# Batch-norm matmul on one core: the stores of seventeen output blocks are issued from ScalarE's queue instead of SyncE's

## The chip, the cores and the metric

One core of a Trainium2 chip runs the kernel. The metric is the device time of one execution in microseconds, the median of three runs. Engines are named as in the profile: PE (TensorE, matmuls), PEld (its weight loads), DVE (VectorE), ACT (ScalarE), POOL (GpSimd), SP (SyncE). An engine's instructions run in the order in which they stand in its queue. A transfer is issued by an instruction in the queue of SP, ACT or POOL, and 16 DMA engines then move the data.

## The reference

```python
y = np.matmul(x, weight)                        # (16, 512, 1024) x (1024, 768)
mean = np.mean(y, axis=(0, 1), keepdims=True)
var = np.var(y, axis=(0, 1), keepdims=True)
y_norm = (y - mean) / np.sqrt(var + eps)
return (gamma * y_norm + beta).astype(np.float32)
```

The input is 8192 rows of 1024 float32; the output is 8192 rows of 768 columns in float32, 25.2 MB. Mean and variance of a column go over all 8192 rows, so no value of a column can be stored before the last row has gone through the matmul for it.

## The kernel before

**Work.** The 768 columns are six column tiles of 128, the rows 16 chunks of 512. x and the weights are loaded as bfloat16 through POOL's queue; DVE turns x so that the contracted dimension lies on the partitions (xT_sb). For some chunks ACT and DVE make a second copy with even and odd elements apart (x_pl, L547). Column tiles 0 and 1 are computed with rows on the partitions (L510) while x comes in. Tiles 2 to 5 are computed with columns on the partitions (L575): chunks 0 to 3 early, the other twelve when x is complete, tile after tile. Eight matmuls fill one PSUM bank with a 128x512 result.

**Eviction.** Each such bank is read twice: DVE takes its statistics (L711), then ACT casts it to bfloat16 in SBUF (y_sb, L715). After that the bank is free for PE. PSUM has eight banks in turn; some hold other things for a time (the spread scale and shift rows a_ps, turned blocks o_ps).

**Finish of a column tile.** When its statistics are complete, DVE and ACT work out scale and shift, and the tile's blocks of 1024 rows are normalised in place, by ACT for tile 2 (L1023), by DVE for tiles 3 and 4 (L1026). A block must be turned back to rows before it is stored, in one of these ways:

- "xact": a DMA transpose from SP's queue (L1220), then ACT casts the turned bfloat16 block to float32 in a ring buffer in SBUF (L1232), then a store of 512 KB (L1202). Thirteen blocks of tiles 2 and 3.
- "pe": PE transposes the block 128x128 at a time into a PSUM bank (L1044, placed between matmuls), ACT copies it to float32 in the ring (L1210), then the same store (L1202). Four blocks of tile 4.
- "raw": the block is turned before normalisation by a DMA transpose (L1106), DVE multiplies it by the spread scale row (L1174), POOL adds the shift row (L1178), and SP stores it (L1182). Six blocks. For each tile with raw blocks the rows are spread by DVE (L1141, L1142) and by four small and three larger copies (L1145), on POOL or ACT as the planner chooses, then ACT puts them into a PSUM bank (L1158).
- Tiles 0 and 1 go out over L937, L942 and the store L946, all without a turn.

The tables in the code count column tiles from 0; the functions below serve tiles 2, 3 and 4.

**Tail.** The last block of tile 4 is held back (L1252, L1255). Tile 5 ends with two half chunks (L753); its statistics are closed at once, ACT takes the root (L1311), DVE normalises (L1348), PE turns (L1044), ACT copies to o_sb (L1361) and SP stores (L1364): 4 MB in eleven stores.

**Order.** Nothing of the order is left to a compiler. Every piece of work is a Task with a priority, a table of engines with two times (how long it occupies the engine, and when its result is there), its dependences and its buffers. `arrange` (L122) plays these times forward: it takes the engine that can begin first and gives it the ready task with the lowest priority number, and a task with several possible engines goes where it can begin first. `slack` is added to the time at which a task counts as ready. Transfers go through a model of the DMA engines with a list of landings for each queue (`Wires`, L98), which lets at most eight be under way on a queue. The instructions are then emitted in the order found, and each engine keeps it (`seq`, L293). So a changed time or engine of one task can move other tasks, also on engines that the change does not name. Waits are made from the data: an instruction waits on semaphores for what it reads or overwrites.

The functions with the stores of this change are `col_block` and those in it, quoted here as they stand before.

Of the kernel before, what the change touches and what calls it, by code (L numbers as in the profile page):

```python
# [227 lines left out]
def kernel(  # L228
# [19 lines left out]
    P = 128  # L248
# [44 lines left out]
    def seq(bi):  # L293

        ins = bi.ins
        prev = last.get(ins.engine)
        if prev is not None:
            tc.add_manual_dep(
                ins, prev,
                mybir.DependencyInfo(mybir.DependencyClass.NoSync, mybir.DependencyReason.DATA),  # L300
                reason="order",
            )
        last[ins.engine] = ins.name
        return bi
# [51 lines left out]
    def task(prio, engines, emit, deps=(), lock=False, **kw):  # L356
        t = Task(prio, engines, emit, deps, **kw)
        t.lock = lock
        tasks.append(t)
        return t  # L360

    def dve(occ):
        return {"DVE": (occ, occ + 0.09)}

    def act(occ):
        return {"ACT": (occ, occ + 0.11)}
# [8 lines left out]
    STORE, XBAR = 1 / 350.0, 1.25  # L375

    def piece(slot):
        return ring[:, slot.at:slot.at + slot.words]
# [69 lines left out]
    for kind, n, *n1 in order:  # L448
# [12 lines left out]
        if m0 == M // 2:  # L461
            affine_loads = affine = task(t, {"SP": (5.0, 7.0)}, load_affine, [x_ready[m0 // CH - 3, 0, JW]])
        slot = Slot(rings, rows // 32 * KQ // 2)
# [4 lines left out]
            dma=(rows * K * 4 / 1024 + 384 * also) * PER_KB * 1.024, takes=[slot])  # L468
# [4 lines left out]
        for i in range(rows // QR):  # L473
            c, q = divmod(m0 // QR + i, QPC)
            for j0, j1 in ((0, JW // 2), (JW // 2, JW)) if m0 < CH else ((0, JW),):
# [4 lines left out]
                    uses=[slot] if new else [slot, x_slot[c]], takes=[x_slot[c]] if new else [])  # L480
# [204 lines left out]
    def y_of(nt, c):  # L685
        return y_col.setdefault((nt, c // GY), Slot(ys))

    def y(nt, c, n=1):
        group = y_of(nt, c).y.rearrange("p g m -> p (g m)")
        return group[:, c % GY * CH:(c % GY + n) * CH]  # L690
# [328 lines left out]
    def norm(nt, c, n=1):  # L1019
        def emit(eng):  # L1020
            part = y(nt, c, n)
            if eng == "ACT":
                seq(nc.scalar.activation(  # L1023
                    part, part, AF.Identity, bias=shift[:, nt:nt + 1], scale=scale[:, nt:nt + 1]))
            else:
                seq(nc.vector.tensor_scalar(  # L1026
                    part, part, scale[:, nt:nt + 1], shift[:, nt:nt + 1],
                    op0=ALU.mult, op1=ALU.add))
        return emit

    def turn_block(prio, nt, m0, count, deps, uses):

        bank = Slot(banks)
        todo = []

        def step():
            if not todo:
                o_ps = psum.tile([P, count, P], bf16, tag="b")
                bank.tile = o_ps
                for s in range(count):  # L1040
                    c, i = divmod(m0 // P + s, RT)
                    todo.append((o_ps[:, s], y(nt, c)[:, i * P:(i + 1) * P]))
            dst, src = todo.pop(0)
            seq(nc.tensor.transpose(dst, src, ident))  # L1044

        def emit(eng):
            for _ in range(emit.task.count):
                step()

        emit.step = step  # L1050
        t = task(prio, pe(0.0555 * count), emit, deps, takes=[bank], uses=uses)
        emit.task = t
        turns[t] = [count, count]
        return t, bank
# [136 lines left out]
    def col_block(nt, c, due, fin_task, held=False):  # L1191
        yslot = y_of(nt, c)
        keeps = [col_end[nt, c + i][1] for i in range(GY)]
        count = GY * RT
        slot = Slot(rings, count * P)
        m0 = c * CH

        def dst():
            return out_flat[m0:m0 + count * P, nt * P:(nt + 1) * P].rearrange("(s p) n -> p s n", p=P)

        def store(eng):
            seq(ENG[eng].dma_start(dst(), slot.o))  # L1202

        a = task(due, act(1.144) if nt == GA else dve(0.45), norm(nt, c, GY), [fin_task] + keeps, nt > GA, uses=[yslot])
        if MODE[nt][c // GY] == "pe":
            b, bank = turn_block(due + 0.5, nt, m0, count, [a], [yslot])

            def copy(eng):
                slot.o = piece(slot).rearrange("p (s n) -> p s n", n=P)
                seq(nc.scalar.copy(slot.o, bank.tile))  # L1210

            d = task(due + 1.0, act(0.905), copy, [b], takes=[slot], uses=[bank])
            task(due + 1.2, {"SP": (0.38, 0.4)}, store, [d], dma=count * P * P * 4 / 1024 * STORE * 1.024,
                 uses=[slot])
            return b
        t_slot = Slot(rings, count * P // 2)

        def xbar(eng):
            t_slot.o = piece(t_slot).bitcast(bf16).rearrange("p (s n) -> p s n", n=P)
            seq(nc.sync.dma_start_transpose(t_slot.o, y(nt, c, GY)))  # L1220

        b = task(due + 0.5, {"SP": (1.4, 1.4)}, xbar, [a], dma=XBAR,
                 takes=[t_slot] + ([slot] if MODE[nt][c // GY] == "xact" else []), uses=[yslot])
        if MODE[nt][c // GY] == "xpool":
            def store_x(eng):
                seq(nc.gpsimd.dma_start(dst(), t_slot.o))

            task(due + 1.2, {"POOL": (0.93, 0.93)}, store_x, [b], dma=1.69, uses=[t_slot])
        else:
            def convert(eng):  # L1230
                slot.o = piece(slot).rearrange("p (s n) -> p s n", n=P)
                seq(nc.scalar.copy(slot.o, t_slot.o))  # L1232

            d = task(due + 1.0, act(0.9), convert, [b], uses=[slot, t_slot])
            d.slack = 1.0
            task(due + 1.2, {"SP": (0.38, 0.4)}, store, [d], dma=count * P * P * 4 / 1024 * STORE * 1.024,
                 uses=[slot])
        return b

    def held_block(nt, c, due, fin_task, last_mm, root_task):  # L1240
# [27 lines left out]
    for nt in range(GA, NT - 1):  # L1268
        if nt == NT - 2:
            for i, c in enumerate(LATE):  # L1270
                part_chunk(c, clock[0] + 0.0 + 4.0 * i, {"DVE": (0.63, 0.7), "ACT": (1.05, 1.1)},
                           i == 0, 4.0 / 4, [col_end[NT - 3, late[-1]][1]])
        for c in CHUNKS[nt]:
            for jws in halves if nt > GA or c > EARLY + 2 else [[jw] for jw in range(JW)]:
                col_unit(nt, c, jws)
        for c in RAW.get(nt, ()):
            if c >= EARLY:
                raw_turn(nt, c, clock[0])
        f = finish_tasks(nt)
        start = clock[0] + 3.0  # L1280
        if nt in RAW:
            raw_spread(nt, f)
        for i in range(C // GY):
            if (nt, GY * i) in raw:
                raw_block(nt, GY * i, start + STEP[nt] * i + RAWDUE[nt])
                continue
            if nt == NT - 2 and C // GY - HELD <= i:
                held.append((nt, GY * i, f))
                continue
            col_block(nt, GY * i, start + STEP[nt] * i, f)  # L1290
# [48 lines left out]
    for c, r0, rows in ends:  # L1339
        due = E + 2.0 + 0.6 * c  # L1340
# [4 lines left out]
        for i in range(n):  # L1345
            def norm_part(eng, c=c + i, r0=r0, rows=min(rows, CH)):
# [5 lines left out]
                              uses=[y_of(nt, c + i)]))  # L1352
        m0 = c * CH + r0
        count = rows // P
        b, bank = turn_block(due + 0.6 * (n - 1), nt, m0, count, norms, [y_of(nt, c + i) for i in range(n)])
        slot = Slot(xts)
# [6 lines left out]
        def store(eng, slot=slot, m0=m0, count=count):  # L1363
# [4 lines left out]
        d = task(due + 0.6 * (n - 1), act(0.05 + 0.107 * count), copy, [b], takes=[slot], uses=[bank])  # L1368
        task(due + 0.6 * (n - 1), {"SP": (0.6, 0.6)}, store, [d], dma=count * P * P * 4 / 1024 * STORE * 1.024,
             uses=[slot])  # L1370
# [41 lines left out]
```

## Time and profile before

| What | Value |
|---|---|
| Device time, median of 3 runs | 205.82 us (205.68 to 205.83) |
| Profiled execution: span from the first to the last instruction | 204.1 us |
| Mean granted TensorE clock over the span | 0.979 |
| PE busy | 189.3 us (93%), 1210 instructions |
| DVE busy | 159.3 us (78%), 250 |
| ACT busy | 146.2 us (72%), 260 |
| POOL busy | 124.1 us (61%), 150 |
| HBM read and written | 36.71 MB and 25.17 MB |
| Stores of 512 KB from the ring on SP's queue | 37, 3.4 us from issue to landing (median) |
| DMA transposes L1220 on SP's queue | 13, 4.4 us from issue to landing (median) |

The profile is of one execution; for that execution there is the span and no separate device time. The span and the median differ by 1.7 us, which lie before the first and behind the last instruction. A group's row gives line, engine, operation, what is written and read, the count, then busy us and mean ns of one, then the engine's idle time before these instructions and what ended most of it. Instructions that issue transfers on SP or ACT are not counted as busy; they appear in the timeline as SPq rows with their own length, from the end of their waits to the end of the issue. In the windows view each row is a stretch of time with the busy us of each engine and the number of instructions in brackets, then the granted clock, the mean busy share of the DMA engines (over 1 where several packets of one engine overlap) and GB/s.

### The profile page before, as it was taken

The page shows a single profiled execution, that of the slowest core. Times are in us where ns is not written, and L with a number is a line of the kernel's source. Part 1 is how long each engine was busy: PE and PEld are TensorE (multiplying, and loading weights), DVE is VectorE, ACT ScalarE, POOL GpSimd, SP SyncE. Part 2 cuts the span into 40 slices and gives each one's busy share as a digit, 9 for nine tenths or more (in the row PEclk, how much of TensorE's full clock was granted, in tenths as well). Part 3 has the DMA queues.
Part 4 walks back from the last instruction along what each step waited for, and adds up shares of the span by engine and source line. Part 5 has one row for each costly group of instructions (what it writes and reads, how often), then busy time and mean ns, then how long its engine had stood idle before and what let it go on. Part 6 is the DMA issues. An engine that isn't in the chain of part 4 may idle for free.

```text
span 204.1 us, 3510 instructions
## 1 busy us (share of the span) xinstructions
PE 189.3 (93%) x1210; PEld 114.5 (56%) x1210; DVE 159.3 (78%) x250; ACT 146.2 (72%) x260; POOL 124.1 (61%) x150
## 2 busy tenths in 40 slices
PE   7969999999999999999999999999999999997900
PEld 3457554657488888777865444444444445544600
DVE  4031879999999999969989998987999878657900
ACT  2001461368989999899978766999998959956950
POOL 7776954877499989997403999389613312940000
PEclk9999999999999999999999999999999999999965
DMA  4999999999999999999686899899999999999998
GB/s 71 172 199 196 176 196 196 196 197 197 190 193 197 197 196 196 196 197 195 103 181 200 297 339 336 248 301 328 295 322 227 336 303 274 347 343 310 310 347 253
DMA packets 98562, 48.74 MB, mean 239 GB/s; under 512 B 24304, under 2 KB 98032, under 8 KB 98544
## 3 DMA queue, kind: packets, MB, share of 16 engines
q0 software_dynamic: 34624, 18.36, 65.5%
q1 hardware_dynamic: 63920, 30.16, 52.6%
q8 instruction: 9, 0.15, 0.3%
q14 instruction: 9, 0.07, 0.1%
HBM read 36.71 MB, written 25.17 MB: 303 GB/s over the span
## 4 chain that ended last, share of the span: by engine, by line
PE 86%; ACT 3%; DMA 3%; POOL 2%; issue 1%; ACTq 0%; DVE 0%; POOLq 0%
PE y_ps L575 54%; PE y_ps L510 24%; PE y_ps L814 4%; ACT o_sb L1361 3%; DMA ring<-in_x_dram 3%; PE o_ps L1044 1%; POOL ring L403 1%; POOL w_sb L387 1%; PE y_ps L753 1%; PE a_ps L903 1%; PE o_ps L1074 0%; ACTq L1407 0%; PE idle_ps L591 0%; PE tot_ps L871 0%; ACT ring L1252 0%
## 5 line engine op out<-in xcount | busy, mean ns | idle before, releaser
L575 PEld LDWEIGHTS <-w_sb 128*128 128x128 bf16 x520 | 50.3, 97 | 57.6
L575 PE MATMUL y_ps<-xT_sb,w_sb 128*128 128x512 bf16 (+1 forms) x272 | 59.3, 371 | 0.0
L575 PE MATMUL y_ps<-x_pl,w_sb 128*128 128x512 bf16 x248 | 57.4, 379 | 0.0
L403 POOL DMA_DIRECT2D ring<-in_x_dram x76 | 47.2, 626 | 14.4 <-DMA ring<-in_x_dram 5.5
L510 PE MATMUL y_ps<-w_sb,xT_sb 128*128 128x256 bf16 x448 | 50.6, 273 | 1.7 <-DMA ring<-in_x_dram 1.6
L510 PEld LDWEIGHTS <-xT_sb 128*128 128x128 bf16 x448 | 43.5, 98 | 9.4 <-DVE xT_sb L435 2.9
L435 DVE STREAM_TRANSPOSE xT_sb<-ring 128x1024 f32<-128x1024 f32 (+1 forms) x29 | 31.2, 1111 | 14.1 <-DMA ring<-in_x_dram 13.9
L711 DVE BATCH_NORM_STATS2 stats<-y_ps 128x6 f32<-128x512 f32 x46 | 30.9, 687 | 7.7 <-PE y_ps L575 7.2
L715 ACT CAST y_sb<-y_ps 128x512 bf16<-128x512 f32 x51 | 29.0, 593 | 10.4 <-DVE stats L711 6.3
L547 ACT COPY x_pl<-xT_sb 128x1024 bf16<-128x1024 bf16 x32 | 32.8, 1063 | 1.7 <-DVE xT_sb L435 1.7
L942 POOL TENSOR_TENSOR ring<-ring,sum 128x1024 f32<-128x1024 f32 (+1 forms) x11 | 23.8, 2188 | 14.9 <-ACT y_ps L724 10.9
L659 ACT ACTIVATE sq_sb<-y_ps 128x512 f32<-128x512 f32 x28 | 16.3, 610 | 16.2 <-PE y_ps L510 15.9
L666 POOL TENSOR_TENSOR sum<-sum,sq_sb 128x512 f32<-128x512 f32 x20 | 25.6, 1278 | 3.0 <-ACT sq_sb L659 1.7
L662 DVE TENSOR_TENSOR sum<-y_ps,sum 128x512 f32<-128x512 f32 x28 | 18.9, 675 | 6.3 <-ACT sq_sb L659 5.3
L672 ACT CAST y_sb<-y_ps 128x512 bf16<-128x512 f32 x28 | 16.3, 594 | 8.2 <-DVE sum L662 8.0
L1178 POOL TENSOR_TENSOR ring<-ring,sum 128x1024 f32<-128x1024 f32 x6 | 14.8, 2477 | 9.8 <-issue 8.5
L937 DVE TENSOR_TENSOR ring<-y_sb,a_ps 128x1024 f32<-128x1024 bf16 (+1 forms) x16 | 16.7, 1079 | 0.1
L1044 PE MATMUL o_ps<-ident,y_sb 128*128 128x128 bf16 x104 | 13.1, 221 | 1.6 <-DVE y_sb L1348 1.5
L1232 ACT CAST ring<-ring 128x1024 f32<-128x1024 bf16 x13 | 13.8, 1063 | 0.6 <-DMA ring<-y_sb 0.6
L1145 POOL COPY sum<-sum 32x256 f32<-32x256 f32 (+1 forms) x17 | 5.8, 340 | 13.4 <-DVE sum L1142 6.5
L428 DVE STREAM_TRANSPOSE xT_sb<-ring 128x2048 bf16<-128x2048 bf16 x6 | 13.5, 2290 | 0.1
L591 PE MATMUL idle_ps<-idle_sb 128*128 128x512 f32 x18 | 9.6, 688 | 1.5 <-DVE idle_sb L316 1.5
(104 smaller groups left out, 153.7 us busy)
## 6 DMA issues: line engine op xcount, KB each, us to landing
out_dram<-ring SPq DMA_DIRECT2D x37, 512.0 KB, 3.4
ring<-in_x_dram POOLq DMA_DIRECT2D x52, 256.0 KB, 8.8
out_dram<-o_sb SPq DMA_DIRECT2D x6, 512.0 KB, 4.7
ring<-in_x_dram POOLq DMA_DIRECT2D x16, 128.0 KB, 5.9
w_sb<-in_weight_dram POOLq DMA_DIRECT2D x8, 192.0 KB, 6.2
out_dram<-ring SPq DMA_DIRECT2D x6, 256.0 KB, 3.0
ring<-in_x_dram POOLq DMA_DIRECT2D x4, 192.0 KB, 7.8
out_dram<-o_sb SPq DMA_DIRECT2D x3, 256.0 KB, 2.5
```

The source lines that it names most:

```text
L403: bi = seq(nc.gpsimd.dma_start(x_bf[32 * i:32 * i + 32], src[:, :, KQ * i:KQ * (i + 1)]))
L435: seq(nc.vector.transpose(dst, src[:, :, jw0:jw1]))
L510: seq(nc.tensor.matmul(y_ps[:, s], x_of(c, jw, e, t * P, (t + 1) * P), w_sb[:, jw, e, 0:NA], start=(s == 0 and jw == 0 and e == 0), stop=( ...
L547: seq(nc.scalar.copy(dst, pairs) if eng == "ACT" else ENG[eng].tensor_copy(dst, pairs))
L575: seq(nc.tensor.matmul(y_ps, w_sb[:, jw, e, nt * P:(nt + 1) * P], moving(c, jw, e, q0 * QR, q1 * QR, parted), start=(jw == 0 and e == 0 an ...
L659: seq(nc.scalar.activation(sq_sb[:, 0:n], slot.tile[:, 0:n], AF.Square))
L662: seq(nc.vector.tensor_add(sum1, slot.tile[:, 0:n], sum1))
L666: seq(ENG[eng].tensor_add(acc, acc, state["sq"][:, 0:n]))
L711: seq(nc.vector.bn_stats(dst, slot.tile))
L715: seq(nc.scalar.copy(y(nt, c), slot.tile))
L937: seq(nc.vector.tensor_mul(slot.o, y_row[c].y[:, s0:s1], aff[0][:, None, :].to_broadcast([P, n, NA])))
L942: seq(ENG[eng].tensor_add(slot.o, slot.o, row[:, None, :].to_broadcast([P, n, NA])))
```

## The change

The stores L1202 of `col_block`, of both the "pe" and the "xact" blocks, are tasks of ACT instead of SP: 17 in all. Since `store` takes its engine from the planner, `ENG[eng].dma_start` then issues on ACT's queue. The planner's times for it go from (0.38, 0.40) to (0.2, 0.4), and a store counts as ready 0.3 us later than the end of its cast, so that the planner tends to put another instruction between them. The semaphore wait for the cast stays. All other stores and all DMA transposes stay on SP.

```diff
             d = task(due + 1.0, act(0.905), copy, [b], takes=[slot], uses=[bank])
-            task(due + 1.2, {"SP": (0.38, 0.4)}, store, [d], dma=count * P * P * 4 / 1024 * STORE * 1.024,
-                 uses=[slot])
+            e = task(due + 1.2, {"ACT": (0.2, 0.4)}, store, [d], dma=count * P * P * 4 / 1024 * STORE * 1.024,
+                     uses=[slot])
+            e.slack = 0.3
             return b
...
             d = task(due + 1.0, act(0.9), convert, [b], uses=[slot, t_slot])
             d.slack = 1.0
-            task(due + 1.2, {"SP": (0.38, 0.4)}, store, [d], dma=count * P * P * 4 / 1024 * STORE * 1.024,
-                 uses=[slot])
+            e = task(due + 1.2, {"ACT": (0.2, 0.4)}, store, [d], dma=count * P * P * 4 / 1024 * STORE * 1.024,
+                     uses=[slot])
+            e.slack = 0.3
         return b
```

Because the planner places everything anew, the emitted order differs beyond these stores. Against the program before:

- PE: the same kinds of instructions in the same order.
- ACT: 17 stores, each with at least one other instruction between its cast and itself; seven copies L1145 of tile 3 that POOL ran before; one L547 copy fewer.
- DVE: one L547 copy more, and the L547 and L1174 instructions in other places among L711.
- POOL: the seven L1145 copies fewer.
- SP: the 17 stores fewer; the DMA transposes follow each other with less between them.

## The prediction

> **What bounds the kernel now.** I read the page's chain first: it says which engine the end hangs on.
>
> ```profile
> PE 86%; ACT 3%; DMA 3%; POOL 2%; issue 1%; ACTq 0%; DVE 0%; POOLq 0%
> ```
>
> TensorE (PE) has 86% of the span. In the groups the number to see is the last one, the idle time before these matmuls, which is nothing; ScalarE's (ACT's) evictions L715 do wait, and what ends most of that is VectorE:
>
> ```profile
> L575 PE MATMUL y_ps<-xT_sb,w_sb 128*128 128x512 bf16 (+1 forms) x272 | 59.3, 371 | 0.0
> L715 ACT CAST y_sb<-y_ps 128x512 bf16<-128x512 f32 x51 | 29.0, 593 | 10.4 <-DVE stats L711 6.3
> ```
>
> The waits asked for PE alone between 124 and 188 us list nothing. So up to 186.62, where the chain leaves the last matmul L753, PE is the bound. Behind it comes the tail: statistics, root, the last column tile's blocks, their stores. The windows view (busy us of each engine, clock, DMA share, GB/s) shows what bounds that, and how much room ACT has where the moved stores stand:
>
> ```profile
> 133.70:173.50 39.80, 39.80 (x197) 18.36 (x196) 34.70 (x67) 35.86 (x56) 18.03 (x22) 1.00 1.13 298
> 173.50:186.60 13.10, 13.10 (x83) 7.13 (x82) 8.24 (x14) 9.08 (x14) 7.07 (x3) 1.00 1.15 346
> 188.00:192.00 4.00, 3.37 (x40) 2.25 (x40) 3.96 (x14) 3.49 (x8) 0.00 (x0) 1.00 0.88 265
> 192.00:202.00 10.00, 2.09 (x27) 1.35 (x24) 1.64 (x6) 4.67 (x6) 0.00 (x0) 0.68 1.15 347
> ```
>
> From 173.5 to 186.6 and from 192 on the DMA engines move 346 to 347 GB/s, the most they do in any slice of the page's last quarter but for moments; only 188 to 192 is slack. ACT is idle 39.80 - 35.86 = 3.94 us in the first window and 4.02 in the second. PE is busy all of both, so no change of queues can bring 186.62 forward, and a PE stall before it moves the end one for one, since the final stores cannot start earlier than their data.
>
> **What the change takes from SP.** Seventeen stores of 512 KB (L1202). SP does not bound anything by itself. Its rows near the end (start, us, line) show that issuing gets slow when stores pile up:
>
> ```profile
> 175.88 0.37 SPq L1202 DMA_DIRECT2D out_dram<-ring  x1
> 176.31 0.67 SPq L1182 DMA_DIRECT2D out_dram<-ring  x1
> 177.07 3.08 SPq L1202 DMA_DIRECT2D out_dram<-ring  x2
> 180.20 1.88 SPq L1182 DMA_DIRECT2D out_dram<-ring  x1
> 182.17 1.29 SPq L1202 DMA_DIRECT2D out_dram<-ring  x1
> 183.56 1.41 SPq L1182 DMA_DIRECT2D out_dram<-ring  x1
> ```
>
> On SP such a 1 to 2 us issue holds up only the next store, and the DMA engines are full meanwhile: nothing is gained by removing it. Nor is anything lost by the 13 transposes L1220 (1.30 to 2.37 us each) no longer standing behind stores: they can only come earlier. What is late next is the cast on ACT, as now.
>
> The Trainium skill bears on this: "DMA: Bandwidth & Descriptors", section "Issuing engines are not separate DMA queues", says that transfers started from several engines end up on the same 16 DMA engines, and that issuing from more than one saves only issue time. The 346 GB/s agrees with the limit, but no row before has two hardware queues; by that page the gain is nothing, as in my sum.
>
> **What it puts on ACT.** The changed program's order has PE's kinds of instructions unchanged; the 17 stores stand on ACT, nearly always one instruction behind their cast. The planner also moves seven copies L1145 (column tile 3) from POOL to ACT and one L547 copy from ACT to DVE. Net compute: four small copies at 0.25 us (ACT's four L1145 rows fill 1.0 us), three 32x256 copies, which ACT does not run now, between 0.25 (that row) and 0.31 (L1158, 128x256, from its starts to the next starts); I take 0.31, since it has the same length per partition. Minus one L547 at 0.95 (start to start): 1.00 + 0.93 - 0.95 = 0.98 us. DVE has 39.80 - 34.70 = 5.1 us idle for the extra 0.7 us copy and POOL gets freer; without that room the copy's 0.7 us would come on the evictions.
>
> The price of a store on ACT is not in the trace. Every store waits for its own cast, and ACT's sequencer takes what follows only after the issue. From both sides: nothing, if the instruction between hides it all; a gain is excluded, since ACT only gets more to do; 2.22 us, the longest L1202 issue on SP. In between I build it from three rows. The issue itself: the first eleven L1202 issues on SP add up to 5.07 us, 0.46 each (0.37 alone, 0.53 to 0.54 just behind a transpose). The cover:
>
> ```profile
> 133.71 1.05 ACT L1232 CAST ring<-ring 128x1024 f32<-128x1024 bf16 x1
> 134.64 0.60 ACT L715 CAST y_sb<-y_ps 128x512 bf16<-128x512 f32 x1
> 135.12 1.26 ACT L1023 ACTIVATE y_sb<-y_sb,shift,scale 128x1024 bf16<-128x1024 bf16 x1
> ```
>
> The cast ends at 134.76, the next-but-one instruction starts at 135.12: 0.36 us hidden, 0.10 left. Third, company: a store straight behind a transpose takes 0.16 us longer, so a transpose seems still to hold something when SP goes on. If ACT's issue has to wait while SP issues a transpose, the 14 transposes from 128.5 to 170.4 (24.4 us of 41.9, 58%) cost it on average 0.58 x half of 1.74 = 0.51. I take 0.10 + 0.51 = **0.6 us** a store, near the 0.53 median of SP's own 17 issues.
>
> The sum goes where ACT is most needed. These are the L715 that frees a PSUM bank (its eviction ends at 172.93 + 0.58 = 173.51) and the transpose on PE that takes this bank, by the program's waits, at 175.70:
>
> ```profile
> 172.93 0.58 ACT L715 CAST y_sb<-y_ps 128x512 bf16<-128x512 f32 x1
> ...
> 175.70 0.22 PE L1044 MATMUL o_ps<-ident,y_sb 128*128 128x128 bf16 x1
> ```
>
> Its room is 2.19 us, the least of all banks (elsewhere 3 to 9). In the changed order 11 of the 17 stores and the 0.98 us stand ahead of it. ACT comes 0.98 + 11 x 0.6 - 3.94 = 3.64 us later there, if all idle time is used up; minus the room of 2.19, PE stands 1.45 us. The other six stores meet 4.02 us of idle time up to 186.6 and no transposes, so they add nothing at 0.6 (3.6 us). **Sum: span 204.1 + 1.45 = 205.5; 1.7 us lie between the span and the median of 205.82, so 207.3.** The execution profiled has no time of its own besides the span; the runs shown agree within 0.15 us.
>
> At nothing per store, the result is 205.8. With the whole issue in the open (0.37 + 0.51 = 0.88): 0.98 + 9.68 - 3.94 - 2.19 = 4.5, or 210.4. At 2.22 everywhere the same line gives 19 us, which I keep only as the far end.
>
> **Rivals.**
>
> *Hidden (same).* PE stands still only from (3.94 + 2.19 - 0.98) / 11 = 0.47 us per store on. For it: the 0.36 of cover is nearly the bare 0.37 issue. Against: it needs the company of SP's transposes to cost little. Time: 205.6 to 206.2.
>
> *Faster.* With ACT's stores out of SP's queue, the last L1182, issued at 183.56 although POOL was done with that block at 182.05, goes 1.5 us earlier, and the backlog ahead of the final stores shrinks. It decides if those final stores wait behind older ones. The issue table speaks against it: the 128 KB o_sb stores land 2.1 us after issue, the shortest of all stores, and 188 to 192 has room already (265 of 347 GB/s, 0.95 us). At most half of that can come off the end: 205.3.
>
> *Locked out (much slower).* ACT waits for whole transposes or stores of SP at most issues, and the casts behind them hold PSUM banks. At 0.88 it is 4.5 us, 210.4; over 1 us per store beyond 211. For it: the slow SP rows above at three stores under way. Against: with two queues each has fewer stores under way. Trainium skill, "Perfetto Trace Analysis", section "DMA Instruction — HWDGE (DVE, Sync)": an issue first waits for a descriptor generator that two sequencers share and lock. By that rule ACT waits out whole transposes, this rival's way; the trace before, with SP alone, cannot show it beyond the 0.16 us.
>
> *Not what it says.* The order shows the 17 stores on ACT, so this has no chance worth a number.
>
> **How the numbers follow.** Forecast (a stall of about 0.4 to 3 us) 0.43; hidden 0.34; locked out 0.16; faster 0.07. Slower by over 0.2% (0.41 us, about what a measurement of this kernel can tell from no change) is 0.43 + 0.16 = 0.59; same 0.34; faster 0.07. The range takes in the hidden case and the 0.88 price: 205.5 to 210.5; outside stay half of locked out and most of faster, under 2 in 10. The slower cases alone: 206.3 to 210.5.
>
> **What would show it.** Right: ACT's DMA issues of 0.4 to 1.2 us, longer where SP issues a transpose; idle time of L575 or L1044 released by ACT, first near 175; ACT's idle time before 173 gone. Wrong: issues of 0.1 to 0.4 us with ACT still idle near 164 (hidden), or a PE end at 186.6 with a shorter tail (faster). A stall released by DVE or by a transfer instead of ACT would make the reason wrong even if the time were right.

## The result, and the profile after

The changed kernel takes 207.93 us (median of 4 runs, 207.67 to 208.25), the kernel before 205.82 on the same chip (205.68 to 206.06). The ratio is 1.0098 with a 95% interval of 1.0083 to 1.0114: slower by 2.1 us. The profiled executions have spans of 206.2 and 204.1 us, the same difference.

The page's chain of the changed kernel, to be held against the 86% PE and 3% DMA shown before:

```profile
PE 77%; DMA 9%; ACT 4%; POOL 2%; DVE 2%; issue 1%; ACTq 0%; DVEq 0%; POOLq 0%
```

PE's part has shrunk by 9 points and DMA's has grown by 6. It is tempting to read this as a sign of the cause, but it is none: the 6 points are loads of weights (w_sb<-in_weight_dram, 6% in the page's list by line), which end at 18 us, long before the first of the moved stores. The kernel with the new plan and all stores on SP, further below, has 9% too. The next two views look for the predicted price of a store on ACT. This is line L1202 of the changed kernel (durations in ns: minimum, median, maximum), and then ACT's timeline at two of the 17 issues (start, us):

```profile
L1202 ACTq DMA_DIRECT2D out_dram<-ring x17: 378/378/431, 134.9 to 186.7; - x17
```

```profile
134.76 0.60 ACT L715 CAST y_sb<-y_ps 128x512 bf16<-128x512 f32 x1
134.90 0.43 ACTq L1202 DMA_DIRECT2D out_dram<-ring  x1
135.38 1.24 ACT L1023 ACTIVATE y_sb<-y_sb,shift,scale 128x1024 bf16<-128x1024 bf16 x1
```

```profile
145.53 0.29 ACT L990 ACTIVATE std<-mv,eps_sb 128x1 f32<-128x1 f32 x1
145.66 0.41 ACTq L1202 DMA_DIRECT2D out_dram<-ring  x1
145.73 1.03 ACT L547 COPY x_pl<-xT_sb 128x1024 bf16<-128x1024 bf16 x1
```

No issue on ACT takes longer than 0.43 us. The issue at 134.90 runs while L715 still computes; L1023 starts 0.62 us after L715, where before it was 0.48 (134.64 to 135.12). So 0.14 us are in the open, not 0.6. Behind L990 the next copy starts after 0.20 us with a store between the two, as it did without one. The second issue also falls into a transpose that SP is issuing:

```profile
144.94 3.93 SPq L1221 DMA_TRANSPOSE ring<-y_sb  x2
...
156.37 3.28 SPq L1106 DMA_TRANSPOSE r_sb<-y_sb  x1
```

SP is busy with two transposes from 144.94 to 148.87, and ACT's store at 145.66 takes 0.41 us all the same: here ACT does not wait for SP. The Trainium skill, "Perfetto Trace Analysis", section "DMA Instruction — HWDGE (DVE, Sync)", counts a wait for the lock into the time that the profiler shows; 0.41 us beside a median of 0.378 leaves no room for such a wait here. (In two kernels below single issues on ACT do take over 2 us, beside stores of SP.) SP's own transposes do get longer: the one at 156.37 takes 3.28 us to issue, and the longest before took 2.37. From issue to landing (line L1221; L1220 before) they take:

```profile
DMA to landing us min/median/max: 2.9/4.6/7.6
```

Before, the same answer had 3.4, 4.4 and 5.6. ACT's waits from 124 to 190 us (us in total, times, longest) show who meets the late ones:

```profile
ACT ring L1210 <- DMA out_dram<-ring: 4.2, 2, 3.4
ACT ring L1233 <- DMA ring<-y_sb: 2.7, 2, 1.4
```

The casts L1233 wait 2.7 us for transposes (0.6 before), and the casts L1210 wait 4.2 us for a place in the ring that an older store is still reading (0.2 before). The same view for PE lists no wait before the tail. PE's last matmul L753 ends at 187.09 instead of 186.62, and 0.1 us of this was there already at 125 us. The root L1313 comes at 188.83 instead of 187.41, the last store lands at 205.24 instead of 203.15. Of the root's 1.42 us, 0.47 are PE's; the rest is ACT's, which after the wait of 3.4 us for the ring is still busy with older casts when the statistics are ready.

How much has been moved by when shows more. I cut the time into stretches other than those of the prediction, since by 176 us all transposes have landed in both kernels and all that is left to move is stores; the last row reaches over the room that the prediction saw at 188 to 192. Before, then after (length, busy us of PE, PEld, DVE, ACT, POOL; PE clock, DMA share, GB/s):

```profile
136.00:150.00 14.00, 14.00 (x66) 6.32 (x65) 11.91 (x22) 14.00 (x21) 9.59 (x10) 1.00 1.13 320
150.00:176.00 26.00, 26.00 (x141) 12.46 (x139) 22.41 (x45) 22.02 (x36) 8.56 (x12) 1.00 1.16 295
176.00:186.00 10.00, 10.00 (x58) 5.20 (x57) 6.14 (x11) 6.08 (x9) 4.76 (x3) 1.00 1.15 345
186.00:194.00 8.00, 6.43 (x78) 4.42 (x75) 6.85 (x23) 7.10 (x14) 0.00 (x0) 1.00 1.00 300
```

```profile
136.00:150.00 14.00, 13.95 (x66) 6.25 (x65) 11.84 (x23) 13.50 (x19) 9.52 (x10) 1.00 1.11 325
150.00:176.00 26.00, 25.79 (x135) 12.29 (x137) 21.46 (x45) 22.20 (x40) 4.46 (x5) 1.00 1.10 270
176.00:186.00 10.00, 9.95 (x55) 5.00 (x55) 6.97 (x11) 5.78 (x9) 6.61 (x3) 1.00 1.14 343
186.00:194.00 8.00, 5.45 (x55) 4.72 (x54) 6.02 (x21) 7.18 (x15) 0.00 (x0) 0.80 1.04 314
```

Both kernels move the same 48.74 MB in all. From 150 to 176 us the changed one moves 25 GB/s less over 26 us, or 0.65 MB; add 0.07 MB more in the first stretch and 0.02 less in the last, and it is 0.60 MB behind at 186 us. At 347 GB/s, the most that the engines do, this is 1.7 us of work. I call this number the arrears at 186 us; it is worked out for other kernels below in the same way. It is not yet a loss: from 186 to 194 us the kernel before leaves the engines room (300 GB/s), and a kernel with arrears can make them up there. The changed one moves 314 and is still 0.49 MB or 1.4 us behind at 194. What of the 2.1 us this does not explain lies in how the last transfers end (last section). All these figures are from one execution of each kernel.

### The profile page after: what moved, and what is told of

Same layout as the page of the kernel before. It is cut to its first block, busy times and chain, and to the rows that moved or that the text cites. A ratio compares the mean times of both kernels' runs of the same rounds, so it can differ in the third digit from the quotient of the medians.

```text
span 206.2 us, 3483 instructions
## 1 busy us (share of the span) xinstructions
PE 190.0 (92%) x1195; PEld 116.4 (56%) x1210; DVE 159.6 (77%) x251; ACT 147.0 (71%) x266; POOL 121.9 (59%) x143
## 2 busy tenths in 40 slices
DMA packets 98562, 48.74 MB, mean 236 GB/s; under 512 B 24304, under 2 KB 98032, under 8 KB 98544
## 4 chain that ended last, share of the span: by engine, by line
PE 77%; DMA 9%; ACT 4%; POOL 2%; DVE 2%; issue 1%; ACTq 0%; DVEq 0%; POOLq 0%
PE y_ps L575 49%; PE y_ps L510 21%; DMA w_sb<-in_weight_dram 6%; PE y_ps L814 4%; DMA ring<-in_x_dram 3%; ACT o_sb L1363 3%; PE o_ps L1044 2%; POOL ring L403 1%; ACT y_sb L715 1%; POOL w_sb L387 1%; DVE xT_sb L435 1%; PE a_ps L903 1%; ACT ring L1210 0%; PE o_ps L1074 0%; ACTq L1409 0%
## 5 line engine op out<-in xcount | busy, mean ns | idle before, releaser
L575 PE MATMUL y_ps<-xT_sb,w_sb 128*128 128x512 bf16 (+1 forms) x264 | 58.4, 371 | 0.4
L711 DVE BATCH_NORM_STATS2 stats<-y_ps 128x6 f32<-128x512 f32 x46 | 30.6, 685 | 4.6 <-PE y_ps L575 4.6
L547 ACT COPY x_pl<-xT_sb 128x1024 bf16<-128x1024 bf16 x31 | 31.7, 1052 | 1.7 <-DVE xT_sb L435 1.7
L715 ACT CAST y_sb<-y_ps 128x512 bf16<-128x512 f32 x51 | 28.4, 586 | 4.8 <-DVE stats L711 3.2
L672 ACT CAST y_sb<-y_ps 128x512 bf16<-128x512 f32 x28 | 16.0, 602 | 7.6 <-DVE sum L662 7.4
L1233 ACT CAST ring<-ring 128x1024 f32<-128x1024 bf16 x13 | 13.5, 1045 | 3.0 <-DMA ring<-y_sb 2.7
L591 PE MATMUL idle_ps<-idle_sb 128*128 128x512 f32 x18 | 10.6, 747 | 1.5 <-DVE idle_sb L316 1.5
L1174 DVE TENSOR_TENSOR ring<-r_sb,a_ps 128x1024 f32<-128x1024 bf16 x6 | 7.3, 1212 | 5.4 <-DMA out_dram<-ring 2.7
```

What stands on the lines that cost most here:

```text
L547: seq(nc.scalar.copy(dst, pairs) if eng == "ACT" else ENG[eng].tensor_copy(dst, pairs))
L575: seq(nc.tensor.matmul(y_ps, w_sb[:, jw, e, nt * P:(nt + 1) * P], moving(c, jw, e, q0 * QR, q1 * QR, parted), start=(jw == 0 and e == 0 an ...
L711: seq(nc.vector.bn_stats(dst, slot.tile))
L715: seq(nc.scalar.copy(y(nt, c), slot.tile))
```

## The experiments

Three theories stood against each other. Theory 1: the new plan, whose order makes a cast wait for a place in the ring. Theory 2, the prediction's: the time that an issue takes on ACT. Theory 3: two hardware queues, which let stores run among the transposes, so that the casts get their data later.

**The plan and the queue, each alone.** The store function is the only place that differs. With the changed kernel's plan and the stores back on SP:

```diff
-            seq(ENG[eng].dma_start(dst(), slot.o))
+            seq(nc.sync.dma_start(dst(), slot.o))
```

> The changed kernel's plan (order of every engine, places in the ring), with the 17 stores started from SyncE after all. Theory 1, the plan (a cast on ScalarE waits 3.4 us for a place in the ring that an older store still reads): the loss stays, 207.3 to 208.3 us, and the root stands at about 188.8 us of the trace. Theory 2, the issues themselves on ScalarE (0.6 us each): the loss goes, 205.6 to 206.3. Theory 3, two hardware queues that make SyncE's transposes longer (3.05 and 3.28 us instead of at most 2.37): the loss goes, 205.6 to 206.3, and these two transposes are short again.

Measured: 207.3 us against 205.96, ratio 1.0064 [1.0044, 1.0085]. The root is 0.33 us earlier than in the kernel before (as nearly everything is from 20 us on, so this is a shift of the start), and yet the last store lands 0.88 us later. The arrears: 13 GB/s less over 26 us and 8 less over 10 make 0.42 MB, 1.2 us. But of these 0.35 MB are made up from 186 to 194 us (344 GB/s against 300), so they do not explain the end; nearly all of the 0.88 us comes behind 194, where one DMA engine works on alone (last section). So the plan alone costs about two thirds of the loss, and not by way of the root, as theory 1 had it. Theories 2 and 3, which expected no loss here, miss this part. What theory 3 said of the transposes does come: with one queue again, their longest issue is 2.42 us and they land after 4.0 us in the median and 5.6 at most, as before.

With the plan of before and the stores on ACT, at the places that the plan had given them on SP:

```diff
-            seq(ENG[eng].dma_start(dst(), slot.o))
+            seq(nc.scalar.dma_start(dst(), slot.o))
```

> The kernel before with its own plan, and only the engine that starts the 17 stores changed to ScalarE, at the places where the plan had them on SyncE. Theory 1 (the plan): no loss, 205.6 to 206.3 us, root within 0.3 us of before's 187.41. Theory 2 (issues of 0.6 us on ScalarE): 207 to 208. Theory 3 (two queues lengthen transposes): 207 to 208, with transposes of about 3 us in the trace.

Measured: 208.02 us against 205.96, 1.0098 [1.0065, 1.0131]. The root comes 0.93 us later, the last landing 2.0 later, and transposes take up to 8.2 us to land (5.6 before). The queue alone costs as much as the whole change, so theory 1 is not needed. This kernel also has one long issue on ACT, among the last stores, when SP is slow to issue its own (three in 5.88 us from 177.54): it starts at 180.13, takes 2.43 us, and ACT's next instruction waits for nothing else:

```profile
182.60 0.59 ACT L715 CAST y_sb<-y_ps 128x512 bf16<-128x512 f32 x1 [2.01 <-issue]
```

So the issue's price is not always small. The two parts don't add up: 0.64% and 0.98% against 0.98% for both.

**The wait for a place in the ring.** In the changed kernel the third cast L1210 waits 3.4 us. I gave it another place, and in a second kernel the second cast too (`own` then also holds `(4, 8): slice(P, 2 * P)`):

```diff
+    held, own = [], {(4, 10): slice(0, P)}
...
-                slot.o = piece(slot).rearrange("p (s n) -> p s n", n=P)
+                slot.o = (w_sb.rearrange("p jw e n -> p (jw e) n").bitcast(f32)[:, :, own[nt, c]] if (nt, c) in own else piece(slot).rearrange("p (s n) -> p s n", n=P))
```

> The changed kernel; only the third cast L1210 (chunks 10 and 11 of column tile 4) writes into a place of its own (the part of w_sb that column tiles 0 and 1 had) instead of the ring's place that the raw store before it still reads. Theory 1: its wait of 3.4 us is gone, the root comes 1.0 to 1.5 us earlier, and the time is 206.2 to 206.9 us. Theories 2 and 3: no change, 207.6 to 208.2.

> The changed kernel with the second and the third cast L1210 in places of their own in w_sb: takes away the 0.83 us wait of the second as well. Theory 1: 206.0 to 206.8 us, at or up to 0.4 below the kernel with the third alone. Theories 2 and 3: 207.6 to 208.2.

Measured: 208.07 us, 1.0091 [1.0064, 1.0119], and 208.32 us, 1.0106 [1.0074, 1.0138], against 205.96. No gain; but these two are poor tests, as PE's waits of the first show (150 to 187 us):

```profile
PE y_ps L575 <- ACT w_sb L1210: 0.9, 1, 0.9
```

The new place lies among the weights, and the program makes PE's next matmul wait for the cast that writes there, 0.9 us each time, though it reads other columns. So the edit took one wait and put in another: the root stays at +1.45 us (+3.02 in the second kernel, which has two such waits). What speaks against the ring's place as the whole cause is the ledger instead. The long wait ends at 184.15, and the changed kernel was 0.58 MB behind (0.65 less the 0.07 of the first stretch) by 176 us already, 1.7 us of work. What part of the end is due to the wait stays open: it holds up the root, and with it the stores that could use the room from 186 to 194 us.

**Which of the 17 stores cost.** The plan of before again, with only the four stores of column tile 4 on ACT, which come after the last transpose, and then only the 13 of column tiles 2 and 3 (`nc.sync` and `nc.scalar` changed over):

```diff
-            seq(ENG[eng].dma_start(dst(), slot.o))
+            seq((nc.scalar if MODE[nt][c // GY] == "pe" else nc.sync).dma_start(dst(), slot.o))
```

> The kernel before with its own plan; only the four stores of column tile 4, which come after the last transpose, are started from ScalarE. Theory 3 (transposes and stores in two queues hold each other up on the DMA engines): no loss, 205.6 to 206.3 us. Theory 2 (price of an issue on ScalarE): four of the 17, and all on the casts ahead of the root: 206.3 to 207.

> The kernel before with its own plan; only the 13 stores of column tiles 2 and 3, whose blocks come through SyncE's transposes, are started from ScalarE. Theory 3: the whole loss of the 17, 207.5 to 208.5 us, with over 60 engine-us of 256 B packets held between 128 and 176 us (46 before). Theory 2: 13 of 17 of the loss, 207 to 207.6.

Measured: the four take 206.21 us against 206.18, 1.0005 [0.9987, 1.0023]: nothing, although one of their issues takes 2.18 us (at 180.16; it falls for the most part into time in which ACT would wait for statistics). The 13 take 208.94, 1.0139 [1.0117, 1.016]: all of it, and if anything more than the 17. So the stores that run beside transposes are enough for the whole loss. ACT's longest waits in the kernel with the 13, from 124 to 190 us:

```profile
ACT ring L1232 <- DMA ring<-y_sb: 3.9, 3, 3.3
ACT ring L1210 <- DMA out_dram<-ring: 3.2, 1, 3.2
```

and its 13 transposes take this long to land:

```profile
DMA to landing us min/median/max: 2.9/5.6/7.4
```

3.9 us of waiting for transposes instead of 0.6, the longest 3.3 us, because a transpose now lands after 5.6 us in the median instead of 4.4. ACT is 3.2 us late with the L715 that was at 160.75, and the last statistics on DVE and the root come 0.86 us later. How the one leads to the other is in the chain of work (start, us, what) and in PE's waits:

```profile
153.44 7.36 DMA ring<-y_sb
...
170.03 0.23 PE o_ps L1044
```

```profile
PE o_ps L1044 <- DVE y_sb L1026: 0.5, 1, 0.5
```

The transpose that takes 7.36 us holds up the casts on ACT, these the root of column tile 4 (L990), this its normalisation on DVE (L1026), and PE waits 0.5 us for the first block that it is to turn. PE's end is 0.86 us late, of which 0.2 were there at 125 us. In the kernel with all 17 on ACT the same wait is 0.7 us; before, and in the changed kernel, there is none. So with the old plan PE does stand, and for late data. The second of ACT's waits, for a place in the ring, comes behind 176 us; here the root follows PE's end without a delay, so it does not hold up the root.

The arrears at 186 us are 0.53 MB (20 GB/s less over 26 us, 2 less over 10, 1 more over 14), of which 0.25 are made up by 194 us (331 GB/s against 300); the rest, 0.28 MB, is 0.8 us. The last store lands 2.4 us later, so much of the loss lies in the last transfers here too. What the expectation said of held packets did not come: beyond their usual 18 ns, those of 256 B (the transposes') hold engines for 52 us, not 60, and this tells nothing, since kernels with one queue beside the transposes have 39 (before), 55 (the four late stores) and 57 (the plan alone). The 46 given as the figure before had packets of 512 B in it.

**ScalarE's time without a second queue.** Stores on SP, and a copy on ACT at each store's place:

```diff
-            seq(ENG[eng].dma_start(dst(), slot.o))
+            seq(nc.scalar.copy(tot[:, 1], tot[:, 0])); seq(ENG[eng].dma_start(dst(), slot.o))
```

> The kernel before with its own plan and all stores on SyncE, but with a copy of 128x256 words between two parts of an unused tile on ScalarE at each place where the store's issue would stand (17 extra instructions of about 0.4 us). Theory 2: the loss of ScalarE's time without any second queue, 207 to 208.3 us. Theory 3: no loss, 205.6 to 206.4.

Measured: 207.94 us against 206.18, 1.009 [1.0071, 1.0109]. So ACT's time, theory 2's cause, can give such a loss without a second queue; but see how. The first of the copies on ACT's timeline:

```profile
134.62 0.60 ACT L715 CAST y_sb<-y_ps 128x512 bf16<-128x512 f32 x1
135.10 0.43 ACT L1202 COPY tot<-tot 128x256 f32<-128x256 f32 x1
135.41 1.26 ACT L1023 ACTIVATE y_sb<-y_sb,shift,scale 128x1024 bf16<-128x1024 bf16 x1
```

A copy keeps ACT 0.31 us from its next instruction (0.79 instead of 0.48), 17 of them 5.3 us. PE does not mind at all: the last matmul and the root come 0.03 us earlier than before. And yet the span is 1.6 us longer. The windows tell where:

```profile
136.00:150.00 14.00, 14.00 (x66) 6.32 (x65) 10.90 (x20) 14.00 (x23) 9.62 (x10) 1.00 1.08 305
150.00:176.00 26.00, 26.00 (x142) 12.48 (x140) 23.02 (x46) 24.88 (x46) 8.43 (x12) 1.00 1.20 299
176.00:186.00 10.00, 10.00 (x59) 5.21 (x58) 6.23 (x12) 7.70 (x14) 4.74 (x3) 1.00 1.06 318
186.00:194.00 8.00, 6.43 (x73) 5.65 (x71) 6.82 (x23) 6.96 (x14) 0.00 (x0) 0.79 1.12 338
```

PE is busy 50.00 of 50 us, but the DMA engines move 15 GB/s less in the first stretch and 27 less in the last: later casts, later stores, idle DMA engines. With 4 more in the middle, 0.38 MB or 1.1 us are in arrears at 186. But 0.30 MB of them are made up by 194 us, so that only 0.08 MB or 0.2 us are left, and the end is still 1.6 us later: from 203 us on a single DMA engine works (last section). So a kernel whose PE and root are on time can end 1.6 us later, and nearly all of that is in its last transfers. That the late stores bring this about is likely, but no run shows how.

**A second queue without ACT.** The 17 stores on GpSimd's queue (`nc.gpsimd.dma_start`):

> The kernel before with its own plan; the 17 stores are started from GpSimd's queue, so that they are again apart from the transposes but cost ScalarE nothing. Theory 3: a loss as with ScalarE's queue, 207 to 208.5 us (more if GpSimd's issues hold up its adds). Theory 2: no loss, 205.6 to 206.4.

Measured: 213.09 us against 206.18, 1.0349 [1.0328, 1.037]. The transposes take up to 8.6 us to land, as theory 3 has it. But 17 issues of 0.89 us hold up GpSimd too, and the root is 5.9 us late, so the size says nothing about the queue. Inconclusive.

**Time given back to ACT.** The 13 stores on ACT, and the casts ahead of them cut to five eighths; then the same cut with all stores on SP:

```diff
-                seq(nc.scalar.copy(slot.o, t_slot.o))
+                seq(nc.scalar.copy(slot.o[:, 0:5], t_slot.o[:, 0:5]))
```

> The 13 stores of column tiles 2 and 3 on ScalarE, with the plan of before, and each of the 13 casts ahead of them covers only five eighths of its block (the other three eighths of it are left out), about 0.4 us less on ScalarE: the time of an issue is given back. Theory 2 (ScalarE's time): the loss goes, 205.4 to 206.5 us. Theory 3 (two queues): it stays, 207.3 to 209.

> The kernel before, stores on SyncE, with the same 13 casts cut to five eighths: what 13 x 0.4 us of relief on ScalarE gives by itself. Theory 2: a little faster or the same, 205.0 to 206.3 us, since casts come earlier and the DMA engines stand still less. Theory 3: the same, 205.6 to 206.3.

Measured, against 205.86 us: 206.09, 1.0009 [0.9995, 1.0023], and 205.8, 1.0003 [0.9989, 1.0017]. The first kernel's windows:

```profile
136.00:150.00 14.00, 13.95 (x65) 6.32 (x65) 11.94 (x21) 12.29 (x20) 9.46 (x10) 1.00 1.13 326
150.00:176.00 26.00, 25.83 (x139) 12.55 (x140) 22.42 (x44) 20.05 (x36) 8.61 (x13) 1.00 1.16 292
```

With 4.4 us less work on ACT (13 casts of 0.73 us instead of 1.05 to 1.06) the loss of 1.39% is gone, the DMA engines are not in arrears (6 GB/s more over 14 us, 3 less over 26, as much as before over 10), and the relief alone gains nothing. The transposes still take up to 6.8 us to land, and ACT still waits 3.9 us for them; but with the stores on SP and the same short casts it is 6.4 us and 3.4, so casts that are ready early wait with one queue too, at no loss. So the loss passes through ACT, which theory 2 got right and theory 3 as I had put it did not. But the relief, 0.33 us per cast, is several times what most issues show (0.00 to 0.14 us), so it may as well have made room for late transposes.

**The transfers by themselves.** A kernel with nothing but 13 stores of 512 KB and 13 transposes, all independent, in turn from SP; and one with the stores from ACT:

```diff
-        nc.sync.dma_start(out_flat[...], ring[:, i])
+        nc.scalar.dma_start(out_flat[...], ring[:, i])
         nc.sync.dma_start_transpose(t[:, i], y[:, i])
```

> Only DMAs: 13 stores of 512 KB and 13 transposes of the size of L1220, all independent, in turn on SyncE's queue. By the packets' times it needs 13 x 1.5 + 13 x 0.9 = 31 us of all 16 engines, or 13 x (0.53 + 1.75) = 30 us of issuing: 31 to 36 us from first issue to last landing. The companion of the kernel with two queues; the theories differ on that one.

> The same 26 transfers, the stores from ScalarE's queue and the transposes from SyncE's. Theory 3: transposes and stores hold each other up on the DMA engines, so the stream takes at least 2 us longer than with one queue, with more 256 B packets of over twice their usual 18 ns. Theory 2: nothing is lost on the DMA engines, so it takes as long or is shorter.

The transposes' line, with one queue and then with two (issue, ns; issue to landing, us):

```profile
L36 SPq DMA_TRANSPOSE t<-y x13: 1533/2001/2232, 14.8 to 51.0; - x13
...
DMA to landing us min/median/max: 3.6/4.8/5.2
```

```profile
L36 SPq DMA_TRANSPOSE t<-y x13: 1308/3430/4432, 14.8 to 47.8; - x13
...
DMA to landing us min/median/max: 3.3/7.4/10.2
```

First issue to last landing is 43.5 us with one queue (12.41 to 55.93) and 45.1 with two (11.95 to 57.02). Both are well over the 31 to 36 that I had worked out from packets and issues. The difference of 1.6 us is short of theory 3's 2, on one execution each; of the 13312 packets of 256 B, 1777 instead of 1214 take over twice their usual 18 ns, as it has it. What is clear is the wait: with ACT's stores beside it, a transpose lands after 7.4 us in the median instead of 4.8, and its issue takes 3.4 us instead of 2.0. The stores wait as well: 7.2 us instead of 4.5 to land, and ACT's issues get long too:

```profile
L34 ACTq DMA_DIRECT2D out_dram<-ring x13: 378/787/2359, 12.0 to 47.6; - x13
```

No compute engine is involved here. By these medians some 4 transfers are under way at once instead of 3 (my estimate: 26 transfers times their time to land, over the whole time); the longer landings may come from that alone. The Trainium skill, "DMA: Bandwidth & Descriptors", section "Issuing engines are not separate DMA queues", says that transfers of several engines "interleave with each other". These two runs agree, and show what that means for a transfer that somebody waits for.

## Why the prediction was right and wrong

- **The outcome** was right: slower, 207.93 us in a range of 205.5 to 210.5, 0.6 us from the forecast of 207.3. The way there was mostly wrong, so that the time came out so near is luck: a cost that did not come stood in for one that had been put at nothing.
- **The step that failed first** is the price of a store on ACT, "0.10 + 0.51 = 0.6 us". The 0.10 holds (0.00 to 0.14 in the open). The 0.51, a wait for transposes that SP is issuing, does not come in the changed kernel: no issue exceeds 0.43 us, one inside a transpose's issue among them. Where an issue in one of the other kernels did take over 2 us (2.43 and 2.18), it stood among SP's late stores, behind the last transpose, where the prediction had put it at "no transposes, so they add nothing". By the prediction's own condition (0.47 us per store) the stall at 175.70 should then not come, and it doesn't: PE takes its transposes there (now at 175.47) without a wait, and its end moves by 0.5 us, not 1.45.
- **"They can only come earlier"**, of the transposes, was the second failure, and, as far as the runs show, the one that mattered. I looked at SP's queue, where they do get free of the stores, and not at the DMA engines, where the stores now run among them. They land up to 7.6 us after the issue (5.6 before), and the casts on ACT wait 2.7 us for them (0.6 before). That is what takes ACT's time, not the issues.
- **"A PE stall before it moves the end one for one"** left out the other road to the end. The prediction saw that 173.5 to 186.6 and 192 on are saturated, and took this only as a reason why nothing is gained. It also means that what is not moved before 176 us can be made up only in the about 1 us of room at 188 to 192. The changed kernel does not make it up (1.4 us are left at 194 us). And the end can be late without any stall of PE: the kernel with copies on ACT has PE and root on time and ends 1.6 us later.
- **The copies L1145 and the plan.** I priced the planner's moves at 0.98 us of ACT. The plan alone costs 0.64%, without a late root and with only 0.2 us of arrears left at 194 us. Which of its moves does it, and how, was not taken apart.
- **The rivals.** *Hidden* had the issue's price right and the time wrong. *Locked out* expected waits for transposes at the issue; they came at the cast. *Faster* is refuted also for the four late stores, which cost and gain nothing.

What stays open is how the loss of the 13 stores divides between ACT's issues and late transposes. In favour of the transposes: twelve of the issues keep ACT some 0.7 us in all (my sum of the starts), and the last, which stands right behind its cast, some 0.5, while 5.3 us of copies were needed for 0.9%; casts wait 3.9 us for transposes, against 0.5 with the copies; and the chain to PE's wait at 170 us goes through a transpose. Against them: with short casts on SP a wait of 3.4 us costs nothing. Open is also why one DMA engine ends late, which makes up nearly all of the loss with the copies and with the plan alone, and about half of it with the queue alone. No run takes the late transposes away and leaves the stores on ACT, or loads ACT with 0.7 us alone; neither was tried.

## What to carry to other kernels

A second queue does not only save issue time: its transfers run among those of the first, so put on it what nobody waits for, at a time when nobody waits for the rest (the last four stores were free, the 13 beside the transposes cost 1.4%). Where a kernel ends with saturated DMA engines, look also at bytes: a kernel can end later though PE and the last reduction are on time (+1.6 us with the copies). Compare what has been moved at several times up to the last packet, and not at one: here most of what was missing at 186 us was made up by 194 in two kernels that still ended late. And look whether a wait is at the issue, at the landing, or at the place that the landing frees, before giving it a price.

## What the runs showed of the hardware

At the end of several kernels one DMA engine alone is late. This is a part of the end of the kernel with copies on ACT:

```profile
203.00:204.00 1.00, 0.00 (x0) 0.00 (x0) 0.00 (x0) 0.00 (x0) 0.00 (x0) 0.50 0.07 22
```

22 GB/s is a sixteenth of 347: fifteen engines have finished, and one works on for over 1 us. Before, all sixteen end nearly together (346 GB/s up to 202.6 us, 156 in the next 0.2, then nothing). How long it works alone goes with how full the engines were from 186 to 194 us: at 299 to 300 GB/s (before, the four late stores, the short casts with ACT's queue) 0.1 to 0.3 us are lost after 194 (the time to the last packet less that of the bytes left at 346 GB/s), at 314 (the changed kernel) and 321 (the short casts on SP, in an execution 0.9 us above that kernel's median) 0.5 to 0.7, and at 325 to 344 (the queue alone, the 13 stores, the copies, the plan alone) 1.1 to 1.6. With the copies this is 1.6 us against 0.1, which is nearly the whole loss. So the room at 188 to 192 us in the kernel before seems to let a late engine catch up, and arrears that fill this room seem to take that away; this rests on one execution of each kernel, the trace does not name engines, and why one falls behind is not known.

Also unexpected: in the changed kernel the issue of a store on ACT costs its next instruction hardly anything, since it goes on while the instruction ahead of it still computes (0.38 us, of which 0.00 to 0.14 show). That is no rule: an issue right behind its own cast showed some 0.5 us with the 13 stores, one among SP's late stores kept ACT for 2.0 us, and beside transposes without a pause issues took 0.79 us in the median.
